# The order in which a mixer's small products are laid between its projections: runs of at least three K tiles

## The chip, the cores and the metric

The kernel runs on one core of a Trainium2 chip. The metric is the device time of one execution in microseconds (us), as the median of several runs. Five engines work side by side: TensorE (PE, matmuls; its weight loads are listed as PEld), VectorE (DVE), ScalarE (ACT), GpSimd (POOL) and SyncE (SP), which issues DMAs.

## The reference

An encoder trunk of two layers over 512 frames with 1024 channels. Every layer is a macaron block:

```python
for l in range(DEPTH):                                   # DEPTH = 2
    h = h + HALF * _swiglu(_rmsnorm(h, ffn1_norm[l]), ffn1_w_in[l], ffn1_w_out[l])
    xn = _rmsnorm(h, mix_norm[l])
    z = xn @ w_in[l]                                     # one projection, cut into heads and gates
    y_a = _rwkv7_mixer(r, k, v, xw, xa, xg, ...)         # a recurrence over time, 8 heads
    y_b = _mlstm_mixer(mq, mk, mv, mo, mi, mf, ...)      # chunkwise attention with gates, 4 heads
    u = sigmoid(g_a) * (y_a @ br_a[l]) + sigmoid(g_b) * (y_b @ br_b[l])
    h = h + u @ w_out[l]
    h = h + HALF * _swiglu(_rmsnorm(h, ffn2_norm[l]), ffn2_w_in[l], ffn2_w_out[l])
return _rmsnorm(h, final_norm)
```

## The kernel before

Activations lie transposed, channels on partitions and the 512 frames in the free dimension. Every full product is made three times, as high part by high part, high by low and low by high (lines 460 to 462, `product`): one K tile of 128 channels is three matmuls of 128 x 512. A projection has 8 K tiles. Its weights are loaded by `weights` as one 512 KB DMA (`wraw`) and split into `whi` by ACT (line 424) and `wlo` by DVE (line 425), in two pieces of four K tiles; each of them has four buffers. Projections collect in PSUM under the tag `mm` (three buffers), small products under `mx` (five).

A layer runs three stages: a feed-forward part, the mixers, a second feed-forward part. In the mixers stage 46 column tiles of the input projection are made (368 K tiles): 30 for the heads and, as fillers, 16 for the merge gates. Between them lie the small products of the recurrences: matmuls of 16 to 128 rows and columns, and sums over partitions. `Weave` sets that order on PE. Each piece of work is a Python generator, a thread: one for the common columns, four for the four pairs of RWKV heads (`rwkv`), three for the mLSTM (`mlstm_heads`, `mlstm_projections`, `mlstm_gates`), one for the gates (`gates_spilled`, the filler). A thread emits its instructions and yields what it waits for: a lock, a flag, a due time (`"at"`) on the planner's own clock `t`, or a projection (`"proj"`). `run` picks the first thread in the order of ranks that is ready and lets it go on; only if none is ready does it emit one K tile of the current projection and move `t` by its cost, 0.69. `pe` moves `t` for small products, with 0.1 more at each change between the two kinds. When no projection is left, `t` jumps to the next due time. PE then works in exactly that order; the other engines' orders are made by the tile scheduler around it, and each engine works its queue in order.

The chain of one pair of heads is, with the lines of its matmuls: decay and gate (923, 927), sums (481, 482), chunk products (1002), transposes (673), the values (1125), the inverse of the chunk matrices in four steps (1086, 1094, 1102, 1108), `u` (1144, evicted by ACT in line 1147), out in two halves (1156), sums of states (1166), seven steps over the chunks (1175 R, 1178, with a DVE step in line 1181 between two), then two normalising sums (481, 482) with Ln and Exp on ACT (lines 512, 513, each with a load of its function table) and the gate product (1214, 1216). The result `y` goes by DMA to DRAM (`yd`) and comes back as `yh`, `yl` (line 487, 488) for the merge. An mLSTM head has its own: 774 and 781 (four of them), 796, transposes.

Behind the weave the merge multiplies `yh0` to `yh7` by `br`: for each of 8 output tiles first the mLSTM half (`yh4` to `yh7`), then the RWKV half (`yh0` to `yh3`). `yh3` comes from the last pair. These products are no longer in the weave's fixed order; the tile scheduler may lay them between the last small products. Below, "tail" is the end of a mixers stage, from the last steps of the inverse of the last pair to the first product that reads `yh3`.

Of the kernel before, what the change touches and what calls it, by code (L numbers as in the profile page):

```python
# [230 lines left out]
class Weave:  # L231
# [47 lines left out]

    def run(self):  # L280
        trunk = self.trunk
        job = None
        self.threads.sort(key=lambda th: th[0])
        while job or any(not th[3] for th in self.threads):
            th = next((th for th in self.threads if self.ready(th[2])), None)
            if th is not None:
                if th[2][0] == "lock":
                    self.held.add(th[2][1])
                self.resume(th)
                continue  # L290
            if job is None:
                th = next((th for th in self.threads if th[2][0] == "proj"), None)
                if th is not None:
                    job = [th, trunk.weights(th[2][1]), trunk.mm(), 0]
                    th[2] = ("job", None)
                    self.mark(0.0, 1.4)
            if job is not None:
                th, w, ps, k = job
                trunk.product(ps, w, k, trunk.xh[:, k, :], trunk.xl[:, k, :], k == 0, k == KD - 1)
                self.t += self.STEP + (0.1 if self.small else 0.0)  # L300
                self.small = False
                job[3] += 1
                if job[3] == KD:
                    job = None
                    self.resume(th, ps)
                continue
            times = [th[2][1] for th in self.threads if th[2][0] == "at"]
            times += [self.flags[th[2][1]] for th in self.threads if th[2][0] == "flag" and th[2][1] in self.flags]
            self.t = min(times)
# [963 lines left out]
```

## Time and profile before

| | |
|---|---|
| time, median of 3 runs | 2456.25 us (2452.19 to 2456.63) |
| the profiled execution | 2451.83 us, its span 2450.1 us |
| PE busy in the span | 2394.5 us (98%) |
| DVE, ACT, POOL busy | 1306.7, 1054.2, 111.1 us |
| granted TensorE clock, mean | 0.993 of full speed |

The two mixers stages are the stretches in which PE's busy share falls below 100% and in which DVE and ACT are busiest. In the rows below a window's line gives each engine's busy time and number of instructions; a line of waits names who waited and what ended the wait; a line of the timeline merges instructions that stand in a row, and the bracket at its end is the idle time ahead of it.

### The profile page before, as it was taken

How to read it: one execution, taken by the hardware profiler on the slowest of the kernel's cores; microseconds unless marked ns; L12 is line 12 of the kernel's file. 1: busy time of each engine (PE TensorE's matmuls, PEld its weight loads, DVE VectorE, ACT ScalarE, POOL GpSimd, SP SyncE). 2: the span in 40 equal slices, each digit the busy share in tenths (PEclk: the TensorE clock that was granted, in tenths of full speed). 3: DMA queues.
4: the chain of work that ended last, by engine and by line, in shares of the span. 5: the costliest groups of instructions: out<-in, count | busy, mean ns of one | idle time of the engine just before them, and what ended most of it. 6: DMA issues, size and time to landing. Idle time of an engine off the chain costs nothing.

```text
span 2450.1 us, 33539 instructions
## 1 busy us (share of the span) xinstructions
PE 2394.5 (98%) x13138; PEld 1945.7 (79%) x13138; DVE 1306.7 (53%) x2341; ACT 1054.2 (43%) x1795; POOL 111.1 (5%) x147
## 2 busy tenths in 40 slices
PE   9999998999999999999999999989999999999997
PEld 7888886787787888888888888867777868888886
DVE  5444347776766644444444434487677665444333
ACT  5333336555645443333343333465566454333322
POOL 0000010000000100000000000100000001000012
PEclk9999999999999999999999999999999999999998
DMA  4332342322344422233322323423223444322332
GB/s 157 98 101 95 108 121 85 106 77 84 105 140 146 137 96 95 95 95 101 97 95 95 103 93 112 129 72 101 81 83 105 148 128 134 98 95 95 94 100 82
DMA packets 114751, 256.13 MB, mean 105 GB/s; under 512 B 39808, under 2 KB 43008, under 8 KB 114592
## 3 DMA queue, kind: packets, MB, share of 16 engines
q1 hardware_dynamic: 113968, 252.35, 33.1%
q8 instruction: 103, 1.69, 0.3%
q10 hardware_dynamic: 624, 1.64, 0.2%
q14 instruction: 56, 0.46, 0.1%
HBM read 230.88 MB, written 23.07 MB: 104 GB/s over the span
## 4 chain that ended last, share of the span: by engine, by line
PE 62%; DVE 3%; ACT 2%; DMA 1%; issue 0%; DVEq 0%; POOL 0%; ACTq 0%; SPq 0%; POOLq 0%
PE mm L460 20%; PE mm L462 19%; PE mm L461 19%; DMA yd<-avr 0%; PE mx L673 0%; DMA t<-yd 0%; PE mx L1156 0%; DVE wlo L425 0%; PE mx L781 0%; PE mx L796 0%; DMA t<-mats 0%; PE mx L1144 0%; ACT L512 0%; ACT L513 0%; PE mx L1102 0%
## 5 line engine op out<-in xcount | busy, mean ns | idle before, releaser
L424 ACT CAST whi<-wraw 128x512 fp32r<-128x512 f32 (+1 forms) x800 | 486.1, 610 | 1058.1 <-PE mm L461 1001.9
L460 PE MATMUL mm<-xh,whi 128*128 128x512 f32 x2160 | 862.7, 399 | 11.0 <-ACT whi L424 10.9
L425 DVE TENSOR_TENSOR wlo<-wraw,whi 128x512 fp32r<-128x512 f32 (+1 forms) x800 | 555.8, 697 | 580.9 <-ACT whi L424 573.1
L462 PE MATMUL mm<-xh,wlo 128*128 128x512 f32 x2160 | 845.8, 392 | 4.9 <-DVE wlo L425 4.7
L461 PE MATMUL mm<-xl,whi 128*128 128x512 f32 x2160 | 844.7, 391 | 0.0
L460 PEld LDWEIGHTS mm<-xh,whi 128*128 128x128 f32 x2160 | 407.5, 189 | 105.9 <-ACT whi L424 12.6
L462 PEld LDWEIGHTS mm<-xh,wlo 128*128 128x128 f32 x2160 | 407.3, 189 | 93.6 <-DVE wlo L425 7.2
L461 PEld LDWEIGHTS mm<-xl,whi 128*128 128x128 f32 x2160 | 407.7, 189 | 82.6 <-issue 1.2
L460 PE MATMUL mm<-hh,whi 128*128 128x512 f32 x704 | 273.9, 389 | 0.0
L461 PE MATMUL mm<-hl,whi 128*128 128x512 f32 x704 | 273.9, 389 | 0.0
L462 PE MATMUL mm<-hh,wlo 128*128 128x512 f32 x704 | 273.9, 389 | 0.0
L461 PEld LDWEIGHTS mm<-hl,whi 128*128 128x128 f32 x704 | 132.2, 188 | 27.6
L462 PEld LDWEIGHTS mm<-hh,wlo 128*128 128x128 f32 x704 | 132.2, 188 | 27.5
L460 PEld LDWEIGHTS mm<-hh,whi 128*128 128x128 f32 x704 | 132.2, 188 | 27.2
L539 DVE TENSOR_TENSOR t<-mm,rstd 128x512 f32<-128x512 f32 x88 | 60.9, 692 | 138.7 <-PE mm L462 127.7
L543 DVE TENSOR_TENSOR t<-mm,t 128x512 f32<-128x512 f32 x88 | 60.9, 692 | 130.1 <-PE mm L462 127.8
L508 POOL TENSOR_TENSOR acc<-acc,t 128x512 f32<-128x512 f32 x36 | 47.9, 1330 | 1194.3 <-ACT t L506 1180.1
L541 ACT ACTIVATE t<-t 128x512 f32<-128x512 f32 x88 | 55.8, 634 | 29.4 <-DVE t L539 29.3
L488 DVE TENSOR_TENSOR hl<-t,hh 128x512 fp32r<-128x512 f32 x88 | 61.0, 693 | 9.6 <-ACT hh L487 2.0
L487 ACT CAST hh<-t 128x512 fp32r<-128x512 f32 x88 | 54.7, 622 | 24.6 <-DVE t L543 24.6
L495 ACT ACTIVATE xh<-h,vec 128x512 fp32r<-128x512 f32 x48 | 34.6, 723 | 44.9 <-DVE h L555 33.7
L460 PE MATMUL mm<-yh,whi 128*128 128x512 f32 x128 | 50.5, 400 | 2.5 <-DVE gb L640 1.6
(243 smaller groups left out, 2066.7 us busy)
## 6 DMA issues: line engine op xcount, KB each, us to landing
wraw<-wi SPq DMA_DIRECT2D x94, 512.0 KB, 3.5
wraw<-f2i SPq DMA_DIRECT2D x88, 512.0 KB, 3.3
wraw<-f1i SPq DMA_DIRECT2D x86, 512.0 KB, 3.3
wraw<-f1o SPq DMA_DIRECT2D x32, 512.0 KB, 3.7
wraw<-f2o SPq DMA_DIRECT2D x32, 512.0 KB, 3.5
gd<-t SPq DMA_DIRECT2D x32, 256.0 KB, 4.1
wraw<-br SPq DMA_DIRECT2D x16, 512.0 KB, 3.7
wraw<-wo SPq DMA_DIRECT2D x16, 512.0 KB, 3.3
```

Of the source, the lines that this page charges most:

```text
L424: nc.scalar.copy(out=hi, in_=raw)
L425: nc.vector.tensor_tensor(out=lo, in0=raw, in1=hi.bitcast(F32), op=ALU.subtract)
L460: nc.tensor.matmul(ps, lhsT=hi, rhs=xh, start=first, stop=False)
L461: nc.tensor.matmul(ps, lhsT=hi, rhs=xl, start=False, stop=False)
L462: nc.tensor.matmul(ps, lhsT=lo, rhs=xh, start=False, stop=last)
L487: nc.scalar.copy(out=hi, in_=x)
L488: nc.vector.tensor_tensor(out=lo, in0=x, in1=hi.bitcast(F32), op=ALU.subtract)
L495: nc.scalar.activation(out=self.xh[:, i, :], in_=h, func=AF.Copy, scale=gain)
L508: eng.tensor_tensor(out=self.acc, in0=self.acc, in1=sq, op=ALU.add)
L539: nc.vector.tensor_tensor(out=g, in0=pg, in1=self.rstd, op=ALU.mult)
L541: nc.scalar.activation(out=s, in_=g, func=AF.Silu)
L543: nc.vector.tensor_tensor(out=p, in0=pu, in1=s, op=ALU.mult)
```

## The change

`run` counts the K tiles emitted since the last small product. While a projection is under way and that count is 1 or 2, no thread is resumed, ready or not: the next K tile comes first. A thread that emits PE work (its planner's time moves) sets the count to 0. Threads are also held back when what they would do next has no PE work. When no projection is under way nothing is held. Nothing else changes: planner's costs, ranks, fillers, and the arithmetic are the same.

```diff
-        job = None
+        job, run = None, 0
...
             th = next((th for th in self.threads if self.ready(th[2])), None)
-            if th is not None:
+
+            if th is not None and not (job and 0 < run < 3):
                 if th[2][0] == "lock":
                     self.held.add(th[2][1])
+                before = self.t
                 self.resume(th)
+                if self.t > before:
+                    run = 0
                 continue
...
                 self.small = False
+                run += 1
                 job[3] += 1
```

Code behind the change stands four or five lines further down, so line 460 of the kernel before is 465 in the new one, 1144 is 1149, and so on. The text uses the old numbers.

Three places of the built order. First PE in layer 0, in the weave's middle: pair 1's inverse step (1102) and the matmuls of an mLSTM head (774, 781), with a state step of the pair before. Before:

```order
L673 MATMUL mx<-cst,pt_3246 128x128 x4
L460 MATMUL mm<-xh,whi 128x512
L461 MATMUL mm<-xl,whi 128x512
L462 MATMUL mm<-xh,wlo 128x512
L1175 MATMUL mx<-st,gt 64x64 x2
L1178 MATMUL mx<-avr_3173,st 64x64 x2
L774 MATMUL mx<-rc,sel 128x512
L781 MATMUL mx<-qk 128x512
L781 MATMUL mx<-qk 128x384
L1102 MATMUL mx<-t1p,mn_3199 32x32 x16
```

and now:

```order
L465 MATMUL mm<-xh,whi 128x512
L466 MATMUL mm<-xl,whi 128x512
L467 MATMUL mm<-xh,wlo 128x512
L1107 MATMUL mx<-t1p,mn_3199 32x32 x16
L779 MATMUL mx<-rc,sel 128x512
L786 MATMUL mx<-qk 128x512
L786 MATMUL mx<-qk 128x384
L1180 MATMUL mx<-st,gt 64x64 x2
```

The inverse step moved ahead of the head's three matmuls, and three K tiles stand ahead of it.

Second, PE in layer 0's tail: the sums of pair 2 and the last pair's `u`, out and sums of states. Before:

```order
L481 MATMUL mx<-sq,sel 128x512
L482 MATMUL mx<-sl,sel 128x512
L1144 MATMUL mx<-s_3207,mn_3199 64x128 x16
L460 MATMUL mm<-xh,whi 128x512
L461 MATMUL mm<-xl,whi 128x512
L462 MATMUL mm<-xh,wlo 128x512
...
L1156 MATMUL mx<-rbx_3203,s_3207 128x128 x8
L481 MATMUL mx<-sq,sel 128x512
L482 MATMUL mx<-sl,sel 128x512
```

and now:

```order
L1113 MATMUL mx<-mn_3199,t1p 32x32 x16
L465 MATMUL mm<-xh,whi 128x512
L466 MATMUL mm<-xl,whi 128x512
L467 MATMUL mm<-xh,wlo 128x512
L486 MATMUL mx<-sq,sel 128x512
L487 MATMUL mx<-sl,sel 128x512
L1149 MATMUL mx<-s_3207,mn_3199 64x128 x16
L1161 MATMUL mx<-rbx_3203,s_3207 128x128 x8
L1219 MATMUL mx<-sg,mats 128x512
L1221 MATMUL mx<-lx_3092,lw_3088 128x512
L1161 MATMUL mx<-rbx_3203,s_3207 128x128 x8
L1171 MATMUL mx<-s_3207,rbx_3203 64x64 x14
```

The projections' products between these groups are gone from here; they stand further ahead. No product that reads `xh` follows in layer 0 now.

Third, ACT in the same place: `acc` and `avr_3173` are pair 2's normalising, `s_3207` is where `u` of the last pair is evicted to, `avr_3195` the last pair's result, `t_6907` a merge gate. Before:

```order
L1199 ACTIVATE acc<-avr_3173 128x512
L1147 ACTIVATE s_3207<-mx 64x512
L487 CAST sq<-acc 128x512
L1147 ACTIVATE s_3207<-mx 64x512 x3
L424 CAST whi<-wraw 128x512
L1159 COPY avr_3195<-mx 64x4x64
L512 ACT_TABLE_LOAD
L512 ACTIVATE acc<-mx,eps 128x512
L1159 COPY avr_3195<-mx 64x4x64
L513 ACT_TABLE_LOAD
L513 ACTIVATE acc<-acc 128x512
```

and now:

```order
L1204 ACTIVATE acc<-avr_3173 128x512
L492 CAST sq<-acc 128x512
L429 CAST whi<-wraw 128x512
L517 ACT_TABLE_LOAD
L517 ACTIVATE acc<-mx,eps 128x512
L664 ACT_TABLE_LOAD
L664 ACTIVATE t_6907<-t_6907 128x512
L518 ACTIVATE acc<-acc 128x512
L1152 ACTIVATE s_3207<-mx 64x512 x2
L1213 ACTIVATE avr_3173<-avr_3173,vec_108 128x8x64
L1152 ACTIVATE s_3207<-mx 64x512 x2
L1164 COPY avr_3195<-mx 64x4x64 x4
```

The evictions of `u` stood ahead of the table loads and now stand behind them, the last two behind a further step of pair 2.

## Rows read from the trace of the kernel before

**Rows 1.** The page: the span, and the line of busy time of the engines.

```profile
span 2450.1 us, 33539 instructions
...
PE 2394.5 (98%) x13138; PEld 1945.7 (79%) x13138; DVE 1306.7 (53%) x2341; ACT 1054.2 (43%) x1795; POOL 111.1 (5%) x147
```

**Rows 2.** Windows: length, busy us (instructions) by engine, granted TensorE clock, DMA share, GB/s.

```profile
122.00:183.00 61.00, 61.00 (x271) 50.52 (x270) 25.91 (x39) 21.11 (x34) 0.00 (x0) 1.00 0.31 101
...
738.97:763.94 24.97, 24.42 (x202) 18.23 (x200) 13.98 (x29) 15.28 (x26) 1.28 (x1) 1.00 0.50 145
763.94:785.59 21.65, 20.52 (x87) 15.20 (x86) 12.26 (x21) 12.44 (x19) 1.30 (x1) 1.00 0.59 186
1954.11:1977.39 23.28, 21.93 (x223) 16.76 (x219) 14.85 (x30) 14.14 (x24) 1.76 (x1) 1.00 0.37 108
1977.39:1999.82 22.43, 17.80 (x65) 11.93 (x66) 10.88 (x18) 11.88 (x17) 1.29 (x1) 0.92 0.56 171
```

**Rows 3.** PE's waits, layer 0 (four) and layer 1 (three): us, times, longest us.

```profile
PE mx L673 <- ACT t L750: 2.4, 2, 1.5
...
PE mx L1125 <- ACT s L1036: 2.2, 2, 1.8
...
PE mx L1102 <- DVE pt L784: 1.0, 1, 1.0
...
PE mx L1094 <- ACT u L1089: 0.6, 1, 0.6
...
PE mx L673 <- ACT t L750: 2.6, 2, 1.5
...
PE mx L781 <- DVE rbx L1009: 1.7, 1, 1.7
...
PE mx L1094 <- ACT u L1089: 1.0, 1, 1.0
```

**Rows 4.** Timeline of PE, layer 0's tail: start, length, line, tiles, count.

```profile
738.97 0.39 PE L481 MATMUL mx<-sq,sel 128*128 128x512 f32 x1
...
763.94 0.27 PE L1178 MATMUL mx<-avr,st 64*64 64x64 f32 x2
...
767.06 0.39 PE L481 MATMUL mx<-sq,sel 128*128 128x512 f32 x1
...
785.59 0.97 PE L460 MATMUL mm<-yh,whi 128*128 128x512 f32 x3
```

**Rows 5.** Instructions by line and form in the two tails: count | busy us, mean ns.

```profile
L460 PE MATMUL mm<-xh,whi 128*128 128x512 f32 x22 | 9.6, 436 | 0.0
...
L460 PE MATMUL mm<-xh,whi 128*128 128x512 f32 x11 | 4.9, 442 | 0.0
```

**Rows 6.** Timeline of PE around two small groups in layer 0.

```profile
500.71 0.48 PE L460 MATMUL mm<-xh,whi 128*128 128x512 f32 x1
501.02 0.39 PE L461 MATMUL mm<-xl,whi 128*128 128x512 f32 x1
...
501.95 0.40 PE L462 MATMUL mm<-xh,wlo 128*128 128x512 f32 x1
502.28 1.15 PE L1125 MATMUL mx<-s,mn 64*64 64x64 f32 x32
```

**Rows 7.** Timeline of ACT in layer 0's tail: evictions of u, table load, Ln.

```profile
741.99 1.83 ACT L1147 ACTIVATE s<-mx 64x512 f32<-64x512 f32 x3
...
745.43 1.28 ACT L512 ACT_TABLE_LOAD   x1 [0.20 <-PE mx L482]
...
746.72 0.69 ACT L512 ACTIVATE acc<-mx,eps 128x512 f32<-128x512 f32 x1
```

**Rows 8.** Timeline of PE, a state step in layer 1's tail that waits.

```profile
1976.67 0.27 PE L1175 MATMUL mx<-st,gt 64*64 64x64 f32 x2 [0.37 <-DVE st L1181]
```

**Rows 9.** PE's wait in layer 0 and the window behind it.

```profile
637.19 0.32 PE L1125 MATMUL mx<-s,mn 64*64 64x64 f32 x2 [1.78 <-ACT s L1036]
...
638.70:641.90 3.20, 3.20 (x8) 2.52 (x9) 3.01 (x14) 3.16 (x7) 1.28 (x1) 0.51 0.00 0
```

## The prediction

> **What bounds the kernel now.** I read the page first: TensorE (PE) is busy for 2394.5 of 2450.1 us [rows 1]. Matmuls overlap, so that alone does not say it runs at its peak; the windows do. In a feed-forward stage 271 matmuls of 512 columns start in 61.00 us, one each 0.225 us, with the clock granted at 1.00 [rows 2]; a K tile (three matmuls) is 0.68 us. Nothing but fewer matmuls would help there, and the change does not touch those stages. It touches the two mixer stages (some 390 to 790 us, and 1580 to 2005 us), where Weave lays projections (46 column tiles of 8 K tiles, 368 in all, in each layer) between the small products of eight threads. PE works without a break there too, but for waits that the list of PE's waits gives [rows 3]. So each mixer stage lasts as long as its PE work plus what PE idles. The PE work stays; the question is what the new order does to the idle time, in the middle of the weave and at its end.
>
> The end is special. Once the 368 projection K tiles are used up, only the last pair's chain is left (u, two halves of out, sums, seven state steps R, two sums, the gate g), and then its way through DRAM into yh3. Beside it lie only those products of the merge that need neither yh3 nor a fourth PSUM buffer: 21 K tiles by the order, before as after. In layer 0 the stretch from the first of the last two sums of pair 2 (738.97) to the first product that reads yh3 (785.59) takes 46.6 us, and 22 projection K tiles lie in it [rows 4, 5]. In layer 1 I start at the last small step L1108 of the inverse (1954.11); to the same product at 1999.82 it is 45.7 us, with 11 [rows 2, 5].
>
> **What the change removes.** (1) Edges. A product after a small group starts its second matmul 0.31 us after its first (500.71 to 501.02), and the first small matmul comes 0.33 us after the last product (501.95 to 502.28), against 0.225 us: about 0.2 us for a group that is no longer on its own [rows 2, 6]. By the order both layers have 175 small groups between products before and 161 after: 14 x 0.2 = 2.8 us at most. All but four of the 14 lie in the two tails, which I cost whole below; outside: 4 x 0.2 = -0.8 us.
>
> The group ahead of 500.71 is made of transposes on the full array (form 128*128), and its edge costs as much as the edge of the 64*64 group at 502.28 [rows 6]. The Trainium skill, TensorEngine Tiling (Array Packing), Key Properties, says that changing the tiling mode drains TensorE; by it only groups of another tile shape would cost, and the order has 238 such changes before and 229 after, which makes 9 x 0.1 = 0.9 us instead of 2.8. The trace agrees for the 64*64 group and not for the transposes. Either way it is the smaller part of the sum.
>
> (2) Waits in the middle. A third K tile (0.68 us) ahead of L1094 covers its wait for ACT, 0.6 us in layer 0 and 1.0 in layer 1. The 1.0 us before L1102 in layer 0 goes, since L1102 now stands ahead of the head's three matmuls and not behind them. In layer 1 two more K tiles stand ahead of the first transposes of t (1.1 of the 2.6 us), and the head's matmuls no longer follow the chunk products whose DVE evictions held them for 1.7 us [rows 3]. Together 0.6 + 1.0 + 1.0 + 1.1 + 1.7 = -5.4 us. The rest of L673's waits (0.9 + 1.5 us, and 1.5; as many K tiles ahead of them as before) and the 2.2 us of L1125 stay. What new waits the other order makes no row can show: between nothing and 6 us, as much as such waits cost a layer now; I take +1, since the runs are longer and the waits on record were behind runs of one or two.
>
> **What it moves: the tails.** Each small step may now wait for three K tiles, so the last pair comes late and the projections are gone before it needs cover.
>
> Layer 0, from the first sum of pair 2. Of the 22 projection K tiles 18 now lie ahead of it: 18 x 0.68 = +12.2 us. In exchange the stretch shrinks. Its first half (24.97 us, to the last R at 763.94) holds 18 of them; without these and nine edges (1.8 us) 11.0 us of small work are left. After: 11.0, four K tiles that stay (2.7), L1108, which now comes behind the sum (1.2), and idle time that had cover. (a) ACT is in order, and in the new order pair 2's Ln and Exp with two table loads and a gate's tanh stand ahead of u's evictions: 1.28 + 0.69 + 1.28 + twice about 0.6, then two evictions of about 0.6 [rows 7], 5.7 us after the sum's end, of which u itself covers 1.9: 3.8 us idle. (b) The first R waits for DVE after sums, about 0.6. (c) Alone, an R step takes 0.72 us (1976.67 to 1977.39, which contains a wait of 0.37 on DVE) [rows 8]; seven steps are 5.0 us, of which about 2.0 are in the small work: 3.0. Sum 11.0 + 2.7 + 1.2 + 3.8 + 0.6 + 3.0 = 22.3 us. The second half, 21.65 us [rows 2], is latency already (halves, sums, Ln and Exp, two DMAs), and I keep it. So 44.0 instead of 46.6, and layer 0 changes by 12.2 - 1.2 + 44.0 - 46.6 = +8.4 us.
>
> Layer 1, from L1108. All 11 K tiles now lie ahead: +7.5 us. First half 23.28 us, minus 11 projection and two merge K tiles (8.8) and eight edges (1.6): 12.9 small work. After, with idle time: the sum needs the halves of what the last R wrote, 3.1 us behind it (763.94 to 767.06) [rows 4], of which R and L1108 cover 1.4: 1.7; u's evictions two of about 0.6, ACT's table loads come later here: 1.2; 0.6 and 3.0 as above. 19.4 us, and the second half 22.43 [rows 2]: 41.8 instead of 45.7. Change 7.5 + 41.8 - 45.7 = +3.6 us.
>
> (3) Clock. Behind the 2.2 us that PE waits for ACT in two pieces at 637 us the granted clock is 0.51 (1.2 GHz) for 3.2 us, and in the second half of layer 1's tail it averages 0.92, against 1.00 in layer 0's [rows 2, 3, 9]. Layer 0's tail will now have idle stretches as long. Two such stretches of 3.4 us lose 1.7 us each where the chain goes through PE, nothing where it goes through ACT or DVE: 0 to 3.4, I take +2.
>
> Sum: -0.8 - 5.4 + 1 + 8.4 + 3.6 + 2 = +8.8 us. The profiled execution has 2451.83 us (span 2450.1 and 1.7 around it); it would become 2460.6. The median of the runs is 2456.25, 4.4 above the profiled one, so I say 2465.
>
> **Rivals.** *The tail costs less (within 0.2%).* If ACT is early enough, or the tail's second half shrinks with the load on DVE and ACT gone, (a) and the clock fall away: 8.8 - 3.8 - 2 = +3.0, 2459. For it: in layer 1 ACT's order keeps the evictions ahead of the table loads. Against: in layer 0 the order is fixed, and ACT waits in it for the sum.
>
> *Faster.* The longer runs cover all that PE waits for in the middle, 6.2 us in layer 0 and 6.3 in layer 1 [rows 3], and ACT's order in layer 0 does not bite: -12.5 - 0.8 + 4.6 + 3.6 = -5.1, 2451. It decides from the point where the waits saved exceed the 12 us of the tails. The waits that would have to go stand behind the same K tiles as before, so I give it little. A second way is the clock: PE was granted less than full speed behind a wait for ACT (L1125), not behind short runs [rows 2, 9], and lifting two stretches of 3.4 us at half speed would give back 3.4 us in all. The Trainium skill, TensorE: Matmul & The Clock Gate, Loop structure matters more than you think, wants dense blocks of matmuls so that the clock stays up; by that rule longer runs are a gain, but here no row ties the lower clock to run length.
>
> *Much slower.* ACT and DVE queues, reordered as at the end of layer 0, hold PE at several places in the middle (6 instead of 1) and both tails lose the clock: +17, 2473.
>
> *The change does nothing.* Excluded: the order has 84 runs of exactly three K tiles, 27 before.
>
> **How the numbers follow.** Forecast (+5 to +13) 0.60; tail cheaper 0.20; much slower 0.13; faster 0.07. A measurement of this kernel tells about 0.2% (4.9 us) from no change; the forecast and the much slower case lie above it, so slower 0.73, same 0.21, faster 0.06. The range leaves out the faster case and the far end of the slow one: 2457 to 2475.
>
> **What would show it.** In the trace of the changed kernel: PE idle after u in layer 0's tail for some 4 us with ACT in a table load; R steps 0.7 to 0.9 us apart; no projection K tile behind L1108's successor sum in either tail; a granted clock under 1 between some 735 and 800 us; the 0.6 and 1.0 us waits of L1094 gone. It is wrong if the last u of layer 0 still has projections behind it, if the waits in the middle fall by more than 10 us, or if new ones of more than 5 us appear there.

## The result, and the profile after

The changed kernel takes 2477.17 us (median of 5 runs, 2473.73 to 2479.18); the kernel before, run beside it, 2456.63 (5 runs, 2452.19 to 2458.84). The ratio is 1.0085 with an interval of 1.0071 to 1.0098: slower by 20.5 us, where 8.8 were forecast. The sign and the loss in layer 0's tail were foreseen; the time lies 2 us above the range.

The page of the changed kernel, the span and the line of the engines, which answer to [rows 1]:

```profile
span 2475.4 us, 33531 instructions
...
PE 2410.2 (97%) x13138; PEld 1958.6 (79%) x13138; DVE 1306.0 (53%) x2341; ACT 1054.4 (43%) x1795; POOL 110.7 (4%) x147
```

The same 13138 matmuls are busy 15.7 us longer, and PE idles some 10 us more. The profiled execution before is one of its shorter ones (2451.83), so a difference of the two traces is 25.3 us where the medians differ by 20.5. Windows of one whole mixer stage, from the norm's matmul to the first product that reads `uh`, say where it arises. The columns are those of [rows 2]. First the kernel before, layer 0 and layer 1:

```profile
374.82:815.32 440.50, 425.70 (x3179) 336.08 (x3178) 309.17 (x663) 247.09 (x446) 17.63 (x37) 0.99 0.35 106
...
1584.18:2030.00 445.82, 425.97 (x3183) 336.13 (x3182) 318.85 (x677) 252.53 (x454) 18.39 (x36) 0.99 0.34 103
```

and the changed kernel:

```profile
374.77:825.84 451.07, 430.04 (x3180) 339.78 (x3178) 310.22 (x663) 247.51 (x446) 17.80 (x37) 0.97 0.33 103
...
1594.69:2054.34 459.65, 436.87 (x3183) 344.70 (x3182) 317.32 (x677) 252.56 (x454) 17.06 (x36) 0.97 0.32 99
```

Length minus PE busy is PE's idle time. Layer 0 is 10.6 us longer (6.2 idle, 4.3 busy), layer 1 13.8 us (2.9 idle, 10.9 busy); the rest of the program adds 0.9. The forecast had +9 for layer 0 and 0 for layer 1, so layer 1 is the miss. The last column but two shows the second thing to look at: the granted clock, 0.99 before and 0.97 now. By the trace's clock records PE was granted half speed (1.2 GHz) for 20.4 us of the two stages before (10.2 in each) and for 54.6 us now (23.9 and 30.7). Each of these is one execution's figure. In two of the runs below a stage whose order is that of the kernel before has 13.7 us (layer 0) and 17.1 us (layer 1) at half speed in place of 10.2, so a difference of 7 us between two traces says little.

The two tails, cut as in [rows 2] and [rows 5]: from the first sum of pair 2 (layer 0) and from the last small step of the inverse (layer 1) to the last R, and from there to the first product that reads yh3:

```profile
751.49:774.28 22.79, 18.40 (x199) 14.23 (x197) 11.54 (x25) 12.36 (x20) 1.27 (x1) 0.93 0.44 138
774.28:795.67 21.39, 18.46 (x65) 12.05 (x66) 11.06 (x18) 11.93 (x17) 1.29 (x1) 0.84 0.45 137
1978.45:2002.32 23.87, 19.00 (x189) 14.56 (x186) 12.52 (x26) 11.82 (x21) 1.26 (x1) 0.79 0.32 100
2002.32:2023.92 21.60, 18.11 (x66) 12.06 (x66) 10.77 (x17) 11.25 (x17) 1.29 (x1) 0.92 0.50 147
```

And PE's waits between the starts and the tails, layer 0 (five rows) and layer 1 (seven), which answer to [rows 3]:

```profile
PE mx L1130 <- ACT s L1041: 2.2, 2, 1.8
PE mx L678 <- ACT t L755: 2.0, 2, 1.2
PE mm L467 <- DVE wlo L430: 1.6, 1, 1.6
PE mx L932 <- DVE pt L789: 0.9, 1, 0.9
PE mx L1099 <- ACT u L1094: 0.5, 1, 0.5
...
PE mm L467 <- DVE wlo L430: 3.1, 2, 2.6
...
PE mx L1007 <- ACT pt L820: 1.6, 1, 1.6
PE mx L932 <- DVE pt L789: 1.3, 1, 1.3
PE mx L1107 <- DVE pt L789: 1.0, 1, 1.0
PE mx L1149 <- ACT s L1152: 0.7, 1, 0.7
PE mx L1130 <- ACT s L1041: 0.6, 2, 0.4
PE mx L1130 <- ACT s L1152: 0.3, 1, 0.3
```

Most of the waits of [rows 3] that the forecast struck out are gone (L1094 and both L673 and L781 in layer 1, L1102 in layer 0). The 0.6 us of L1094 in layer 0, which was to go, stayed at 0.5. Others stand in the place of those that went, for weights (`wlo`), for evictions and for a buffer that DVE has yet to read. The 1.0 us of L1107 in layer 1 is not one of them. It stood in the kernel before, and the working's 6.3 us for layer 1 counts it, though [rows 3] does not show it:

```profile
PE mx L1102 <- DVE pt L784: 1.0, 1, 1.0
```

### The profile page after: what moved, and what is told of

The parts are those of the page before. It is cut to its first block, busy times and chain, and to the rows that moved or that the text cites. A ratio compares the mean times of both kernels' runs of the same rounds, so it can differ in the third digit from the quotient of the medians.

```text
span 2475.4 us, 33531 instructions
## 1 busy us (share of the span) xinstructions
PE 2410.2 (97%) x13138; PEld 1958.6 (79%) x13138; DVE 1306.0 (53%) x2341; ACT 1054.4 (43%) x1795; POOL 110.7 (4%) x147
## 4 chain that ended last, share of the span: by engine, by line
PE 62%; DVE 2%; ACT 2%; DMA 1%; issue 1%; DVEq 0%; POOL 0%; ACTq 0%; POOLq 0%; SPq 0%
PE mm L465 20%; PE mm L467 19%; PE mm L466 19%; PE mx L1161 0%; PE mx L678 0%; PE mx L1007 0%; PE mx L801 0%; DVE wlo L430 0%; ACT L518 0%; PE mx L1180 0%; DMA t<-mats 0%; DMA yd<-avr 0%; PE mx L786 0%; DMA t<-yd 0%; ACT L517 0%
## 5 line engine op out<-in xcount | busy, mean ns | idle before, releaser
L465 PEld LDWEIGHTS mm<-xh,whi 128*128 128x128 f32 x2160 | 408.9, 189 | 103.5 <-ACT whi L429 11.1
L467 PEld LDWEIGHTS mm<-hh,wlo 128*128 128x128 f32 x704 | 132.2, 188 | 27.3
L465 PEld LDWEIGHTS mm<-hh,whi 128*128 128x128 f32 x704 | 132.2, 188 | 27.3
```

The source lines that it names most:

```text
L465: nc.tensor.matmul(ps, lhsT=hi, rhs=xh, start=first, stop=False)
L467: nc.tensor.matmul(ps, lhsT=lo, rhs=xh, start=False, stop=last)
```

## The experiments

Each is the changed kernel or the kernel before with one edit; all have the arithmetic of the whole kernel, and added products write tiles that are overwritten or not read. Times are medians beside the kernel before on the same chip (2454.6 to 2455.5 in these series). A stage is the window above; "half" is its time at half clock. The changed kernel was not run again in these series, so a difference from it is given as the medians have it and, where that matters, by the distances to the kernel before on the same chip (the changed kernel's is 20.5 us).

| run | us | ratio to before, interval | layer 0: stage, idle, half | layer 1: stage, idle, half |
|---|---|---|---|---|
| before | 2456.6 | | 440.5, 14.8, 10.2 | 445.8, 19.9, 10.2 |
| changed | 2477.2 | 1.0085 (1.0071 to 1.0098) | 451.1, 21.0, 23.9 | 459.7, 22.8, 30.7 |
| rule in layer 0 | 2464.5 | 1.0043 (1.0030 to 1.0056) | 452.7, 20.8, 27.3 | 445.7, 17.6, 17.1 |
| rule in layer 1 | 2466.1 | 1.0049 (1.0036 to 1.0062) | 441.7, 15.0, 13.7 | 457.4, 25.5, 20.5 |
| rule, first 30 projections | 2473.6 | 1.0082 (1.0067 to 1.0096) | 446.1, 18.6, 10.2 | 462.5, 25.0, 34.1 |
| rule, last 16 | 2464.5 | 1.0037 (1.0022 to 1.0052) | 447.5, 18.2, 20.5 | 451.0, 20.2, 27.3 |
| runs of two | 2468.5 | 1.0065 (1.0052 to 1.0077) | 448.6, 21.6, 17.1 | 454.1, 23.6, 20.5 |
| weights ahead | 2473.5 | 1.0078 (1.0064 to 1.0091) | 451.7, 19.8, 30.7 | 456.4, 22.8, 30.7 |

### The rule in one layer alone

```diff
-            if th is not None and not (job and 0 < run < 3):
+            if th is not None and not (trunk.l == 0 and job and 0 < run < 3):
```

and with `trunk.l == 1`.

> The rule of three K tiles holds in layer 0 alone. Own loss (the two mixer stages lose separately, as the trace of the changed kernel has it, about +10 us in layer 0 and +15 in layer 1): +10 us over the kernel before, and layer 1's stage with as much half clock as before (about 10 us in two stretches). One sum (the forecast's terms, +9.5 and -0.7): +9 us. Carry-over (the chip lowers the clock in layer 1 because of what layer 0 did, whatever layer 1's order is): +15 us or more, with stretches of half clock in layer 1 that the kernel before does not have.

> The rule holds in layer 1 alone. Own loss: +15 us over the kernel before, of it about 7 in the tail of layer 1 and 6 ahead of it, and six or more stretches of half clock in layer 1. One sum (the forecast): -1 us, no difference that can be measured. Carry-over: less than +10 us, with two or three stretches of half clock in layer 1.

Measured: +9.5 and +11.1 us, together the change's 20.5. The layers lose separately and nothing is carried over: the stage without the rule keeps its length (445.7 and 441.7). The forecast's sum for layer 1 (-0.1 by its terms, with the clock's +2 in layer 0; -0.7 in the expectation) is refuted by a run of its own. The half clock of the stage without the rule was expected as before and is not (17.1 and 13.7 us, 10.2 before), and the length stays all the same.

### The rule for a part of the weave

A counter of the projections begun (46 in a layer) switches the rule.

```diff
+            if th is not None and not (jobs <= 30 and job and 0 < run < 3):
...
+                    jobs += 1
```

and with `jobs > 30`.

> In both layers the rule holds for the first 30 projections and is off for the last 16. By the order 14 projection K tiles are left at the last u of layer 0 (0 in the changed kernel, 22 before), and none in layer 1. Tails (the loss is the cover that the last pair lacks): layer 0 comes back to within 3 us of before, layer 1 stays at +7 or more; in all about +10 us. Clock (the loss is PE at half speed in the middle of the weave): layer 1 ahead of its tail keeps its +6 us and its stretches of half clock between 1600 and 1800 us, since the rule is on there; in all +10 to +16 us.

> In both layers the rule is off for the first 30 projections and holds for the last 16. At the last u 8 projection K tiles are left in layer 0 and 5 in layer 1. Tails: the two tails lose about as far as their cover is gone, +5 us in layer 0 and +2 in layer 1; in all +7 us. Clock: the middle of both layers is as before (half clock only near 396, 639 and 1608 us), so what is left is the tails' +3 to +8 us, and the sum with the kernel that has the rule for the first 30 is the changed kernel's +20 us.

Measured: +18.5 us for the first 30 and +9.4 for the last 16. The first number is outside both expectations. The second is above both (7, and 3 to 8), though its interval (5.4 to 12.8 us) reaches into them, and the two together are not the 20 us that were expected. Layer 0, whose tail has 14 projection K tiles again, still loses 5.6 us, and layer 1 loses 16.7, more than under the full rule. The loss is made in the middle of the weave as well, not only where the projections end; and the parts don't add up (27.9 against 20.5), as each order has waits of its own.

### Runs of two

```diff
+            if th is not None and not (job and 0 < run < 2):
```

> Runs of at least two K tiles in place of three, in both layers. At the last u 16 projection K tiles are left in layer 0 and 8 in layer 1 (22 and 8 in the kernel before). Delay (small products that wait for a run bunch up, and PE then meets late evictions and drops to half clock; the longer the run the more of it): between the two kernels, +5 to +12 us, with some 30 us at half clock in the two mixer stages (20 before, 54 in the changed kernel). Tails alone: +2 us or less, since layer 1's cover is that of before, and half clock as before.

Measured: +13.9 us, 8.1 in layer 0 and 8.3 in layer 1 by the traces, though the tails have nearly the projections of before. Of the two expectations delay is the right one, with more than its 5 to 12 us (12.8 to 18.9 by the interval) and 37.6 us at half clock in place of some 30. PE's longest waits in the two middles, past the starts, one row of each layer:

```profile
PE mx L1099 <- ACT u L1094: 5.2, 1, 5.2
...
PE mx L1180 <- DVE st L1186: 3.7, 1, 3.7
```

Neither is that long in the kernel before or in the changed one. Nothing in the rule says which small step will be caught.

### Weights ahead

```diff
+    def fetch(self):
+        th = next((th for th in self.threads if th[2][0] == "proj"), None)
...
+        w = self.trunk.weights(th[2][1])
...
+                if job[3] == 4:
+                    early = self.fetch()
```

> The changed kernel, but the next projection's weights are loaded and split while the fourth of the eight K tiles of the one ahead of it has just been emitted, not at its start. The split's lower part (DVE) then stands ahead of the evictions of the small groups between. Weights late (the waits for wlo of 1.6 us at 489 and 2.6 us at 1707, and the half clock behind the second, are part of the loss): these waits go and the time falls by 4 to 7 us, to about 2471. Moved wait (DVE has the same work, so something else waits for it in their place): within 2 us of the changed kernel, with as much PE idle in the mixer stages (21 and 23 us).

Measured: 3.7 us less than the changed kernel, or 1.6 by the distances to the kernel before (18.9 and 20.5): nearer to the moved wait. In the trace the waits for `wlo` are gone from both middles (0.4 us are left), and in layer 1 PE waits as long in all (22.8 us in the stage) for others:

```profile
PE mx L1017 <- ACT s L1162: 3.4, 1, 3.4
...
PE mx L811 <- DVE rbx L1024: 3.0, 2, 2.6
```

Half clock is 61.4 us here, more than the 54.6 of the changed kernel, and the time is not longer for it. So the late weights count for little by themselves. What stands in the changed kernel is a queue on DVE. The wait, on PE, and the ends of what DVE does without a pause meanwhile:

```profile
1706.90 0.79 PE L467 MATMUL mm<-xh,wlo 128*128 128x512 f32 x1 [2.64 <-DVE wlo L430]
1707.49 0.63 PE L465 MATMUL mm<-xh,whi 128*128 128x512 f32 x1
1707.91 0.63 PE L466 MATMUL mm<-xl,whi 128*128 128x512 f32 x1
...
1698.26 0.74 DVE L962 SCALAR_TENSOR_TENSOR rw_kk<-rw_k,k,rw_kk 128x512 f32<-128x512 f32 x1
...
1706.16 0.68 DVE L430 TENSOR_TENSOR wlo<-wraw,whi 128x512 fp32r<-128x512 f32 x1
```

Twelve operations of 0.4 to 0.75 us lie between the two DVE rows, work of at least three threads (a pair's inputs, another pair's inverse, an mLSTM head). PE, which had products to do, waits for the split behind them. The rows behind the wait show the other effect: from one product to the next it is 0.42 us (1707.49 to 1707.91), where it is 0.225 at full clock.

The other long new waits stand behind such queues too. What releases PE comes at the end of a stretch in which its engine has no pause of 0.1 us: 9.8 us of DVE for the `wlo` at 488.7, 8.7 and 9.0 us of DVE for the two L932, 5.6 us of ACT for L1007. For the waits in the middles of the kernel before such a stretch is 0.7 to 5.2 us long. It need not be several threads' work: ahead of L932 6.1 us of it are one thread's chain of short operations (L1067, L1069). And that the rule makes these queues longer is not shown. In the two middles together DVE's stretches of over 5 us add up to 341 us in the kernel before and to 308 in the changed one, ACT's to 136 and 148, and a group of small products takes 1.5 us on PE before and 1.6 now. What the traces show is that PE now arrives at the end of long queues, not that there are more of them.

### Filling the waits

Products of 512 columns into a tile that is about to be written anyway (at the starts, into one that nobody reads) keep PE at work where it would wait.

```diff
+    def fill(self, ps, n):
+        for _ in range(n):
+            self.nc.tensor.matmul(ps, lhsT=self.sel[:, 0, :], rhs=self.xh[:, 0, :], start=True, stop=True)
...
+                self.fill(ps4, 10 if l == 0 and p == 3 and q == 0 and b0 == 0 else 0)
```

> The changed kernel with 16 products of 512 columns added, whose results are overwritten: ten ahead of out in layer 0's tail, where PE waits 3.1 us for ACT, six ahead of the last sum of pair 2 in layer 1, where it waits 0.6 and 0.85 us. They ask for 3.6 us of PE where it has nothing to do. Clock (the half clock of 3.4 us from 761 and of 6.8 us from 1983 comes from these waits and costs time): both stretches go or shrink and the time falls by 2 to 5 us. Clock without a price or not from these waits: the stretches stay, and the time is that of the changed kernel or up to 1 us more.

> The changed kernel with 33 products of 512 columns added (results overwritten), in layer 1 alone and where its trace has a wait of PE: 5 ahead of L932 (1.31 us at 1667.6), 11 ahead of the product that waits for wlo (2.64 at 1706.9), 4 ahead of L1107 (0.99 at 1782.9), 7 ahead of L1007 (1.60 at 1862.5), 6 ahead of the first sum of pair 2 in the tail (0.62 and 0.85 at 1980 to 1982). They are 7.4 us of PE in 8.0 us of waits, and nothing else is moved. Waits lower the clock: the half-clock stretches at 1669, 1706.5, 1785 and 1983 (17 us) go, and the time falls by 4 to 8 us. Small products lower the clock: the stretches stay (the small groups ahead of the waits are the same), and the time is within 2 us of the changed kernel. Clock without a price: the stretches go and the time stays.

> The kernel before with 20 products of 512 columns (results unused) where each layer's fifth or sixth half of weights is late: 0.85 and 4.52 us of waiting at 393 to 398, and 4.71 us at 1610. Waits lower the clock and that costs: the half-clock stretches at 396.4 and 1608.2 (6.8 us each) go, and the time falls by 4 to 7 us. Clock without a price: the stretches go and the time stays within 1 us. Not from waits: they stay.

> The changed kernel with 107 products of 512 columns added (results overwritten or unused), 24 us of PE, at twelve places of both layers where its trace has a wait of PE of 0.9 to 5.4 us and a stretch at half clock behind it, the late weights at the start of both layers included; nothing else is moved. To be compared with the kernel before that has the filling at the starts alone (2453.3) and with the changed kernel (2477.2). Clock (most of what the forecast missed is PE at half speed): half clock in the two mixer stages falls from 55 us to 15 or less, and the time by 8 to 12 us, to about 2467, which leaves what the tails and the new waits cost at full clock. Given back (what PE gains at full clock it waits for again, since DVE and ACT set the pace behind a late eviction): half clock falls as far, and the time by no more than 5 us, to about 2473.

| run | us | ratio to before, interval | layer 0: stage, idle, half | layer 1: stage, idle, half |
|---|---|---|---|---|
| changed, tails filled | 2475.2 | 1.0086 (1.0072 to 1.0100) | 449.9, 18.2, 20.5 | 460.0, 23.3, 27.3 |
| changed, layer 1 filled | 2474.7 | 1.0083 (1.0070 to 1.0097) | 451.5, 21.3, 23.9 | 456.0, 18.6, 13.7 |
| before, starts filled | 2453.3 | 0.9995 (0.9987 to 1.0004) | 441.2, 13.1, 3.4 | 446.2, 15.6, 6.8 |
| changed, all filled | 2474.9 | 1.0080 (1.0066 to 1.0093) | 450.4, 13.2, 6.8 | 459.3, 14.1, 17.1 |

*Half clock comes behind waits, and filling mostly removes it.* Where products were put in, the half clock behind them went: at 761 us in layer 0's tail, at 1669, 1706.5, 1785 and 1983 in layer 1, at 396 and 1608 in the kernel before. At 1669 and 1785 the wait itself did not go: the filling waited 1.33 and 0.99 us and ran behind it, so that what is shown there is full clock with more products of 512 columns behind the wait. Nor does it always go: in the run with everything filled the same place has 6.8 us at half clock again (from 1667.8, behind 1.98 us of waiting). The first run's six products in layer 1 stood ahead of the wrong sum of pair 2, where PE does not wait, and there the half clock stayed (1981.3, 6.8 us).

*In the tail that costs time.* Layer 1's tail is the clearest. The changed kernel, on PE:

```profile
1980.26 0.50 PE L486 MATMUL mx<-sq,sel 128*128 128x512 f32 x1 [0.62 <-ACT sq L492]
1981.62 0.50 PE L487 MATMUL mx<-sl,sel 128*128 128x512 f32 x1 [0.85 <-DVE sl L493]
1982.05 2.83 PE L1149 MATMUL mx<-s,mn 64*64 64x128 f32 x32
1984.80 3.79 PE L1161 MATMUL mx<-rbx,s 128*128 128x128 f32 x16
...
1995.05 0.50 PE L465 MATMUL mm<-yh,whi 128*128 128x512 f32 x1 [1.89 <-ACT yh L492]
```

With six products ahead of that sum (lines stand seven to eleven further down), on PE:

```profile
1982.51 1.66 PE L486 MATMUL mx<-xh,sel 128*128 128x512 f32 x6
...
1984.98 1.96 PE L1160 MATMUL mx<-s,mn 64*64 64x128 f32 x32
1986.97 2.29 PE L1172 MATMUL mx<-rbx,s 128*128 128x128 f32 x16
```

and its window from the last small step to the last R:

```profile
1981.41:2001.22 19.81, 15.99 (x196) 12.08 (x195) 12.48 (x26) 11.91 (x21) 1.26 (x1) 1.00 0.40 118
```

Two waits of 0.6 and 0.85 us had made u take 2.83 instead of 1.96 us and half of out 3.79 instead of 2.29. At a clock of 1.00 the first half takes 19.81 us and not 23.87, and the stage is 3.6 us shorter, though its part ahead of the last u is 1.7 us longer with the filling. A merge product that waits for `yh` in front of the state steps, 1.89 us here, is there in the filled one too (2.13 us). With everything filled the way from u to the sums of states is again 6.46 us at full clock (9.34 in the changed kernel); then the same wait of 2.13 us is followed by half clock, which it was not in the other run, and the first half takes 22.5 us. The time shows less than the tail: with layer 1 filled it is 2.4 us below the changed kernel's, or 1.2 by the distances, where 4 to 8 were expected; with the tails filled it is 2.0 below, or not at all by the distances, where 2 to 5 were expected.

*In the middle little of it comes back as time.* With twelve places filled the half clock falls from 54.6 to 23.9 us (one stretch at 1668 and two in layer 1's tail, at 1992 and 2002, stand there again), and the time by 2.3 us (1.1 by the distances), no more than single runs scatter. "Given back" (no more than 5 us) has the number, "Clock" (8 to 12 us) has not. The mean granted clock of its five runs is 0.993, that of the kernel before beside it 0.992, and it takes 19.4 us longer: nearly all of what the change costs is there without a lower clock. From the norm to the last u, without the tails, half clock falls from 13.7 to 3.4 us in layer 0 and from 17.1 to 6.8 in layer 1, and the lengths are 381.9 us (381.8 in the changed kernel) and 388.5 (387.4). The windows of the two stages with everything filled:

```profile
374.62:824.99 450.37, 437.20 (x3226) 344.58 (x3224) 309.88 (x663) 247.18 (x446) 18.20 (x37) 0.99 0.33 103
...
1593.84:2053.17 459.33, 445.22 (x3245) 349.88 (x3243) 318.79 (x677) 252.35 (x454) 16.75 (x36) 0.98 0.31 100
```

Beside them the kernel before with its starts filled, where the clock is 1.00 and 0.99:

```profile
374.41:815.56 441.15, 428.06 (x3200) 338.17 (x3198) 309.13 (x663) 247.10 (x446) 17.62 (x37) 1.00 0.34 106
...
1584.41:2030.62 446.21, 430.64 (x3204) 340.11 (x3203) 318.81 (x677) 252.25 (x454) 18.39 (x36) 0.99 0.33 103
```

At nearly the same clock the change still costs 9.2 and 13.1 us. The 46 and 61 added products of some 0.226 us are 10.4 and 13.8 us, the 20 in each layer of the other 4.5. Idle plus filling, the time that PE is held, is then 23.6 against 17.6 us in layer 0 and 27.9 against 20.1 in layer 1: +6.0 and +7.8. The rest, 3.2 and 5.3 us, is busy time; half of the 3.4 and 10.3 us more that remain at half clock would be 1.7 and 5.1 us of it.

Against the changed kernel PE's busy time without the filling is 8.7 us less (3.2 and 5.5), and the time that it is held is 7.7 us more (2.5 and 5.1). This fits slow products that stood where PE would have waited for DVE or ACT anyway. It does not prove it: behind eight of the twelve fillings PE finds no wait left, so some of them may have outlasted the wait that they filled.

Between executions of one kernel clock and time do go together. Of the 44 of the kernel before in these series, 16 with a mean clock of 0.991 take 2456.1 us in the mean, and nine with 0.993 take 2451.3. Longer waits would bring about both, so this gives no price for the clock.

One reserve: ahead of L932 and L1107 in layer 1 the filling itself waited, since it writes the buffer that DVE had yet to read, and so it was added to the wait and did not fill it:

```profile
PE mx L488 <- DVE pt L798: 3.0, 2, 2.0
```

Nine products, 2.0 us at most, are on the account of these two runs. Without them the fully filled kernel would, by that estimate, be at 2472.9, still 4 us from the changed one and 17 from before.

*The starts.* The fourth filling run shows the same in the kernel before: 4.5 us of products in the 4.7 us wait at 1610 keep the clock at 1.00, and from there to the first chunk products it takes 22.3 instead of 23.65 us. At the last u of layer 1 nothing of that is left (374.1 us from the norm, 373.8 without the filling), in layer 0 1.2 us; the time is 2.2 us lower with an interval that reaches past zero, where 4 to 7 were expected, though the mean clock of its runs is 0.994 against 0.991.

### The merge in another order

```diff
-            for j in (1, 0):
...
+        for i in range(KD):
+            branch(i, 1)
+        for i in range(KD):
+            branch(i, 0)
```

`branch` is the old body for one half, with four K tiles of weights.

> The changed kernel with the merge's products in another order: the halves that need only yh4 to yh7 for all eight columns first, then the others, each with its own half of the weights (same work). By the order 11 and 12 K tiles of the merge then lie between the last u and the last gate, 5 and 7 in the changed kernel, and more can be had behind it. Cover (the tails' loss is PE without work beside the last pair's chain): PE's idle time between the last u and the last gate (6.2 and 5.1 us) falls and the time with it, by 5 to 8 us. In the way (PE is in order, so a merge product that waits for yh holds the state steps, as for 1.9 us at 1995): no gain, 0 to +3 us.

> The kernel before (no rule of three K tiles) with the merge's products in the other order, as in the run of the changed kernel that fell by 10 us with it. Cover: layer 0's tail has its projections (0.6 us idle between the last u and the last gate), so nothing there; layer 1's has 4.9 us idle, of which half goes, and the first product that reads yh3 no longer holds the rest: -3 to -6 us. Merge order as such (a gain that has nothing to do with the tails' cover): -10 us, as in the changed kernel.

> Both of the last two edits in the kernel before, as a version that may beat both kernels: their sum, -7 to -12 us against the kernel before, if cover and clock each act as those runs assume; 0 to -4 us if only one of them does.

Measured: 2466.8 us, 10.4 less than the changed kernel (8.3 by the distances); in the kernel before 2444.4 us (ratio 0.9957, 0.9945 to 0.9970), 11.1 less; with the filled starts too 2443.6 (0.9955, 0.9943 to 0.9968). The gain is as large without the rule, so "merge order as such" has the number, and it is not only the cover lost by the rule that the new order repairs. Cover has a part in it all the same: between the last u and the last gate PE's idle time falls from 6.2 and 5.1 to 3.6 and 2.5 us in the changed kernel, and in layer 1 of the kernel before from 4.9 to 1.5. The order and the smaller loads of weights changed together and were not tried apart. The rule costs 22.4 us with this merge, 20.5 with the old. Layer 1's tail in the kernel before, from the last u to the last gate and on to the first product of `uh`:

```profile
1957.97:1986.17 28.20, 23.30 (x193) 16.73 (x193) 18.66 (x36) 18.39 (x31) 1.76 (x1) 0.96 0.48 145
1986.17:2030.00 43.83, 42.76 (x182) 33.63 (x181) 28.93 (x47) 17.96 (x29) 1.29 (x1) 0.99 0.37 112
```

and with the other merge:

```profile
1957.67:1986.52 28.85, 27.31 (x217) 20.28 (x216) 18.84 (x37) 18.85 (x32) 1.76 (x1) 1.00 0.48 148
1986.52:2022.59 36.07, 36.07 (x159) 29.64 (x158) 28.11 (x45) 16.38 (x26) 1.29 (x1) 1.00 0.45 143
```

24 more matmuls run in the first window, and PE has no idle time left in the second. This version beats both kernels, the one before by 0.4%. The filled starts add nothing that can be measured, so the 11.8 us of the two edits together lie in the range expected of both, and come from one.

## Why the prediction fell short, step by step

The working split the mixer stages into middle and tail. The same cuts in the two traces, which differ by 25.3 us where the medians differ by 20.5:

| term of the sum | forecast | measured |
|---|---|---|
| layer 0, middle (edges, waits gone, new waits) | -1.5 | +1.6 |
| layer 0, tail | +8.4 | +8.6 |
| layer 1, middle | -3.7 | +6.3 |
| layer 1, tail | +3.6 | +7.3 |
| clock, booked apart | +2 | in the rows above |
| other stages, and the merge behind yh3 | 0 | +1.5 |

**What bounds the kernel.** Right: each layer's stage lasts as long as its PE work plus what PE is held, and the layers add up (9.5 and 11.1 of 20.5).

**Layer 0's tail.** Right in its mechanism, and close in size. The stretch takes 44.2 us (44.0 forecast), the halves 22.8 and 21.4 (22.3 and 21.65). That it comes so close is in part luck: the 44.0 leave the clock out, which was booked apart, and the 44.2 have 10.2 us at half speed in them. ACT's order bites as [rows 7] let expect: u ends at 758.5, and ACT is in two table loads, Ln, a gate's tanh and Exp until 760.96.

```profile
756.56 1.97 PE L1149 MATMUL mx<-s,mn 64*64 64x128 f32 x32
761.59 3.39 PE L1161 MATMUL mx<-rbx,s 128*128 128x128 f32 x16 [3.06 <-ACT s L1152]
...
756.61 1.28 ACT L517 ACT_TABLE_LOAD   x1
757.91 0.69 ACT L517 ACTIVATE acc<-mx,eps 128x512 f32<-128x512 f32 x1
758.61 1.28 ACT L664 ACT_TABLE_LOAD   x1
...
760.96 1.19 ACT L1152 ACTIVATE s<-mx 64x512 f32<-64x512 f32 x2
```

3.06 us idle, 3.8 forecast, since PE goes on with the first of the two evictions that were counted. No projection is left behind u, the R steps are 0.72 to 1.06 us apart, and the clock falls to half from 761 and from 774.7 on, as listed under what would show it.

**The waits that go.** Nearly right: 6.8 us are gone (1.0 of L1102 and 0.5 of L1094 and L673 in layer 0; 1.0 of L1094, 2.6 of L673, 1.7 of L781 in layer 1), 5.4 were forecast. L673 in layer 1 gave all of its 2.6 us and not 1.1, L1094 in layer 0 next to nothing of its 0.6. The edges (-0.8) are too small to be found again.

**The new waits: the step that failed.** "Between nothing and 6 us ... I take +1." Measured, from the waits above: 2.5 us in layer 0 (`wlo` 1.6, L932 0.9) and 7.4 in layer 1 (`wlo` 3.1, where 0.2 stood before, L1007 1.6, L932 1.3, L1149 0.7, L1130 0.9), 9.9 in all and beyond the upper bound. The working's own sign of being wrong, "new ones of more than 5 us", is there. Products at half clock may hide more, which at full clock would wait instead; the filled run fits that and does not prove it. The reason given for +1, that longer runs cover more, looks at the run of K tiles ahead of a wait. The five new waits of 0.9 us and more end with the last of 5.6 to 9.8 us that DVE or ACT work without a pause, and a run of three K tiles is 2.0 us. Runs of two and the weights ahead show that the waits fall now here, now there, and that to take one away moves it. The much slower rival named just this ("ACT and DVE queues, reordered ..., hold PE at several places in the middle", 2473) and was given 0.13; it is nearest to what happened, in its lost clock in layer 1's tail too, and the time is still 4 us above it.

**Layer 1's tail and the clock.** The tail without its clock was nearly right: 19.81 us for the first half in the filled run, 19.4 forecast, and 40.3 to yh3's product (1981.38 to 2021.71), 41.8 forecast. What failed is that the waits of 0.6 and 0.85 us ahead of the sum, counted as idle time, also brought half speed to u and out, where PE is the chain: 4 us. The clock term of +2 had two stretches, in layer 0's tail; there were two in it and three in layer 1's, and five more in layer 1's middle (before, one). That it costs where the chain goes through PE and nothing where it goes through ACT or DVE, as the working said, fits layer 1's tail; the second part was not tried by itself.

**The faster rival's rule.** The Trainium skill, TensorE: Matmul & The Clock Gate, Loop structure matters more than you think, wants a loop nest in which matmuls stay back to back, and its bad case is a long DMA wait between every two. The waits here are shorter and on DVE and ACT, and the trace agrees in kind: 84 instead of 27 runs have three K tiles, but PE's idle time in the two stages rose from 34.7 to 43.8 us, and the time at half clock from 20.4 to 54.6 us. Longer runs with longer waits between them are not what the rule asks for.

**Still open.** Why the rule brings PE to the ends of long queues is not known: which thread's delay makes which of the new waits was not traced back, and each order that was run (four rules and the weights ahead) has others. And of the 3.2 and 5.3 us of busy time added at nearly equal clock, what the remaining half speed does not explain (all but 1.7 and 5.1) has no name.

## What to carry to other kernels

To hold ready small steps back until a run of large products is full does not only delay them: it moves the places at which PE needs an eviction, and here the new places lay behind 5.6 to 9.8 us of unbroken work on the engine that evicts, which then sets the pace. When waits are counted that an edit removes, count the queue of the evicting engines in the new order as well, and take as the bound for new waits at least what the removed ones cost. Before clock loss is booked at half the time spent at half speed, ask what PE would do at full speed there: on the last pair's chain it cost 4 us, while with everything filled 31 us less at half speed brought 1 to 2 us.

## What the runs showed of the hardware

Half speed came behind waits as short as 0.99 us, or 0.62 and 0.85 us in a row, with small groups around them, and products of no use put in there mostly kept the clock at 1.00. But a wait does not always bring it down. The same place in the same order, in the kernel before and in the one with the other merge, whose weave has the same order up to there. The step on PE behind its wait of 0.99 us, before:

```profile
1767.78 1.19 PE L1102 MATMUL mx<-t1p,mn 32*32 32x32 f32 x32 [0.99 <-DVE pt L784]
```

and with the other merge:

```profile
1766.06 1.19 PE L1105 MATMUL mx<-t1p,mn 32*32 32x32 f32 x32 [0.99 <-DVE pt L787]
```

The same 3.4 us of the two spans behind it, before:

```profile
1768.30:1771.70 3.40, 3.40 (x40) 2.61 (x37) 0.97 (x2) 1.11 (x4) 0.25 (x1) 1.00 0.01 2
```

and with the other merge:

```profile
1768.30:1771.70 3.40, 3.40 (x16) 2.25 (x15) 0.77 (x2) 0.62 (x1) 0.00 (x0) 0.50 0.00 0
```

The clock is 1.00 in the one and 0.50 in the other; the kernel before has no half speed anywhere between 1615 and 1983 us. So a single trace tells where the clock can fall, not how often it does.
